# Three rounded products for one full-fp32 product of probabilities and values in a two-layer transformer kernel

## The chip, the core and the metric

The kernel runs on one core of a Trainium2 chip, in one launch. The metric is the device time of that launch in microseconds (us). Engines are named as in the profile: PE (matrix products), PEld (its weight loads), DVE, ACT, POOL and SP (which issues nearly all DMAs here).

## The reference, cut to what matters

Two layers of a hybrid backbone act on 1024 latent and 256 context tokens, width 1024, in fp32. Each layer normalises, projects into three parallel groups of heads (latent attention with 6 heads, a state-space model, windowed attention with 6 query and 2 key-value heads), concatenates and projects back, then runs a gated MLP with a short convolution. The change touches the product of probabilities and values in the two attentions:

```python
s = jnp.einsum('bqhd,bkhd->bhqk', qb, keys).astype(F32) * (MLA_QK ** -0.5)
p = jax.nn.softmax(s, axis=-1).astype(vals.dtype)
return jnp.einsum('bhqk,bkhd->bqhd', p, vals)
...
p = jax.nn.softmax(jnp.concatenate([s_sink, s_ctx, s_band], axis=-1), axis=-1).astype(v.dtype)
out = (jnp.einsum('bngrql,blgd->bnqgrd', p[..., 1:1 + n_ctx], v_ctx)
       + jnp.einsum('bngrqk,bnkgd->bnqgrd', p[..., 1 + n_ctx:], vb))
```

## The kernel before, in words

Tokens are 10 tiles of 128 (8 latent, 2 context) or 3 chunks (512, 512, 256). Nearly all large products are made of three passes in a rounded fp32 type (`mm3`, L88): each operand is held as a rounded part (hi) and the rest (lo), and hi·hi, hi·lo and lo·hi are accumulated. `split` (L124) makes the pair: ACT copies into the rounded type, DVE subtracts. The one large product that is a single full-fp32 matmul is that of probabilities and values, called av.

Per layer the order is: projections, state inputs (the loop that writes `us`, before L1839), latent attention, windowed attention, output projection, MLP.

*Latent attention* runs over 6 heads x chunks (L1851). `mla_prep` (L1436) loads a head's keys (`kn`, two buffers), queries and values (`v1`, straight into a tile whose 65th column is one, so that av also gives the softmax's denominator), transposes keys and queries on PE, splits them and takes row maxima on DVE. `mla_steps` (L1531) is one step per key tile: three score passes on PE into a PSUM tile `s` (three buffers), the exponential on ACT into `p` (fp32, four buffers), and a closure that does the av product. The closures wait in the list `pend`, so the product of a step is issued two steps later. Between steps, generators are advanced by a share: preparation of the next unit, the state-space work (`s5`, L1103, whose due times are weighed by a meter, and which is spread over five sixths of the steps), the modulation rows, and then the setup of the windowed attention (`swa_setup`, L1566, and `swa_prep`, L1621). Layer 0 has 6 x (10 + 10 + 2) = 132 steps, layer 1 has 6 x 20 = 120.

*Windowed attention* (`swa_steps`, L1723) works the same way on 384 columns (3 query heads x 128 tokens): 84 steps in layer 0, 76 in layer 1. Its setup loads masks, keys, values and queries; the tag `n2` has two buffers. During it, the mixed inputs of the output projection are loaded and split (`mix_loads`, L1765), and the first output weights (`wo_loads`, L1787; two sets in layer 0).

POOL only does the power of the normalisations (`rsqrt_pool`, L206) and a few memsets. The framework gives each engine its instructions in an order of its own choice near the program's order, and inserts the semaphores; a tile of a tag with n buffers waits until the tile n before it is no longer used. Elementwise and ACT instructions carry the line of a helper (L55), products L86, transposes L96, so groups are told apart by the names of the tiles: `p<-s`, `sp<-s` the exponentials, `av<-p,v` and `av<-sp,sv` the products, `s` the scores, `b` preparation and state space, `u`, `d`, `dx` the MLP, `o` the output projection.

Of the kernel before, what the change touches and what calls it, by code (L numbers as in the profile page):

```python
# [18 lines left out]
T = TL + TX  # L19
# [13 lines left out]
def trunk(ctx, tc, x, c, ctxt, c_ctx, w_mod, b_mod, norm1, w_in, q_lora_g, w_uq, kv_lora_g, w_ukv,  # L33
# [54 lines left out]
    def mm3(out, L, R, start, stop):  # L88
        mm(out, L[0], R[0], start, False)
        mm(out, L[0], R[1], False, False)  # L90
        mm(out, L[1], R[0], False, stop)

# [660 lines left out]
    for l in range(2):  # L753
# [662 lines left out]

        v1s, khs = [], []
        for i in range(2):
            v1 = ap.tile([128, NT, 65], F32, name=f"v1_{i}")
            G.memset(v1[:, :, 64:65], 1.0)  # L1420
            v1s.append(v1)
# [14 lines left out]
        def mla_prep(h, ci):  # L1436
# [3 lines left out]
            if ci == 0:  # L1440
                kn = ap.tile([128, NT, 96], F32, tag="kn", name="kn", bufs=2)
# [3 lines left out]
            if ci == 0:  # L1445
                v1 = v1s[h % 2]
                nc.sync.dma_start(out=v1[:, :, 0:64], in_=vd[h].rearrange("t p d -> p t d"))
# [3 lines left out]
                for t4 in range(0, NT, 4):  # L1451
# [6 lines left out]
                    yield  # L1458
# [72 lines left out]
        def mla_steps(h, ci):  # L1531
# [4 lines left out]
            if h % 2 == 0 and ci == 0:  # L1536
                pair["num"] = ap2.tile([128, T], F32, tag="num", name="num", bufs=2)
                pair["den"] = ap2.tile([128, T], F32, tag="den", name="den", bufs=2)
# [3 lines left out]
            for kt in kts:  # L1542
# [5 lines left out]
                p = ap.tile([128, 512], F32, tag="p", name="p", bufs=4)  # L1548
                act(p[:, :n], ps[:, :n], AF.Exp, scale=96.0 ** -0.5)

                def av(kt=kt, p=p):
# [3 lines left out]
                    mm(av[0:65, :n], v1[:, kt, :], p[:, :n], kt == kts[0], kt == kts[-1])  # L1555
# [10 lines left out]
        def swa_setup():  # L1566
# [3 lines left out]
            mask = swp.tile([128, 2, 128], F32, name="mask")  # L1570
            nc.sync.dma_start(out=mask, in_=k_mask)
            mask_r = swp.tile([128, 2, 128], F32R, name="mask_r")
            V.tensor_copy(mask_r, mask)
            ident_r = swp.tile([128, 128], F32R, name="ident_r")
            V.tensor_copy(ident_r, ident)
            bandm = swp.tile([128, 3, 128], F32R, name="bandm")
            V.tensor_copy(bandm[:, 0, :], mask[:, 1, :])
            ts(bandm[:, 1, :], ones, 0.0)
            V.tensor_copy(bandm[:, 2, :], mask[:, 0, :])
# [10 lines left out]
            swa.update(mask_r=mask_r, ident_r=ident_r, bandm=bandm, sink=sink, sinkrow=sinkrow)  # L1590
            qbs = []
            for i in range(2):
                qb = swp.tile([128, 1536], F32R, name=f"qb_{i}")
                V.tensor_copy(qb[64:128, :], mask[64:128, 0, 0:1].to_broadcast([64, 1536]))
# [3 lines left out]
            for kv in range(2):  # L1598
                k2 = swp.tile([128, 12, 2, 64], F32, tag="n2", name="k2", bufs=2)
                nc.sync.dma_start(out=k2[:, 0:NT], in_=skd[kv].rearrange("t p z d -> p t (z d)"))  # L1600
                v1 = swp.tile([128, NT, 65], F32, name=f"sv1_{kv}")
                G.memset(v1[:, :, 64:65], 1.0)
# [620 lines left out]
```

## Time and profile before

| | us |
|---|---|
| median of 3 runs | 3303.49 (3299.19 to 3305.27) |
| the profiled execution | 3301.99 |
| its span, first to last instruction | 3300.2 |
| busy PE / DVE / ACT / POOL | 3213.9 / 2206.6 / 1165.6 / 108.5 |

The profile is one execution. Its own time lies 1.5 us below the median of the runs. PE's matmuls are pipelined and their ends are modelled, so starts tell more than durations. A matmul in full fp32 appears as two records, each with its own weight load. The four stretches of attention in this execution: latent attention of layer 0 from 297.6 to 671 us (A0) and of layer 1 from 2053 to 2366 (A1), windowed attention from 671 to 788 (B0) and from 2366 to 2470 (B1).

### The profile page before, as it was taken

How to read it: one execution, taken by the hardware profiler on the slowest of the kernel's cores; microseconds unless marked ns; L12 is line 12 of the kernel's file. 1: busy time of each engine (PE TensorE's matmuls, PEld its weight loads, DVE VectorE, ACT ScalarE, POOL GpSimd, SP SyncE). 2: the span in 40 equal slices, each digit the busy share in tenths (PEclk: the TensorE clock that was granted, in tenths of full speed). 3: DMA queues.
4: the chain of work that ended last, by engine and by line, in shares of the span. 5: the costliest groups of instructions: out<-in, count | busy, mean ns of one | idle time of the engine just before them, and what ended most of it. 6: DMA issues, size and time to landing. Idle time of an engine off the chain costs nothing.

```text
span 3300.2 us, 42307 instructions
## 1 busy us (share of the span) xinstructions
PE 3213.9 (97%) x16150; PEld 2577.4 (78%) x16150; DVE 2206.6 (67%) x3987; ACT 1165.6 (35%) x2110; POOL 108.5 (3%) x99
## 2 busy tenths in 40 slices
PE   7999899999999999999999999999999999999999
PEld 4997566677888888888888898556668788888888
DVE  6657887775787766666666845987554756555565
ACT  4532444564232222222222453445562322222221
POOL 0220000000000000000000122000000000000000
PEclk9999899999999999999999999899999999999999
DMA  8534221434312222222211445111323111111111
GB/s 267 130 96 105 87 72 45 125 94 152 96 61 62 73 68 76 64 66 74 68 61 45 127 110 142 29 44 35 90 73 119 33 52 58 45 39 58 52 39 58
DMA packets 405731, 263.15 MB, mean 80 GB/s; under 512 B 173455, under 2 KB 378393, under 8 KB 405529
## 3 DMA queue, kind: packets, MB, share of 16 engines
q1 hardware_dynamic: 404882, 260.20, 27.2%
q8 instruction: 127, 2.08, 0.3%
q14 instruction: 75, 0.61, 0.1%
q10 hardware_dynamic: 647, 0.26, 0.0%
HBM read 207.41 MB, written 50.66 MB: 78 GB/s over the span
## 4 chain that ended last, share of the span: by engine, by line
PE 83%; DVE 10%; DMA 3%; ACT 2%; issue 1%; SPq 1%; POOL 1%; DVEq 0%; ACTq 0%; POOLq 0%
PE u L86 33%; PE d L86 11%; PE av L86 7%; PE o L86 5%; PE dx L86 5%; PE f L86 5%; PE s L86 5%; PE tk L86 5%; PE b L86 4%; PE b L96 2%; DVE cm L55 1%; DVE mx L55 1%; DMA raw<-md 1%; DVE al L55 1%; POOL rinv L102 1%
## 5 line engine op out<-in xcount | busy, mean ns | idle before, releaser
L86 PE MATMUL u<-ah,wh 128*128 128x512 f32 (+1 forms) x1760 | 649.7, 370 | 4.0 <-ACT ah L55 2.2
L86 PE MATMUL u<-al,wh 128*128 128x512 f32 (+1 forms) x1760 | 649.0, 369 | 1.7 <-DVE al L55 1.7
L86 PE MATMUL u<-ah,wl 128*128 128x512 f32 (+1 forms) x1760 | 648.4, 368 | 0.0
L55 ACT ACTIVATE wh<-raw 128x1024 fp32r<-128x1024 f32 (+3 forms) x184 | 189.3, 1036 | 739.8 <-PE d L86 292.1
L55 DVE SCALAR_TENSOR_TENSOR cv<-u,par,cv 128x511 f32<-128x511 f32 (+2 forms) x616 | 326.0, 555 | 133.5 <-ACT cv L55 128.4
L86 PEld LDWEIGHTS u<-ah,wh 128*128 128x128 f32 x1760 | 331.9, 189 | 60.5 <-ACT ah L55 3.1
L86 PEld LDWEIGHTS u<-al,wh 128*128 128x128 f32 x1760 | 332.2, 189 | 58.2 <-DVE al L55 2.8
L86 PEld LDWEIGHTS u<-ah,wl 128*128 128x128 f32 x1760 | 332.2, 189 | 55.2
L55 DVE TENSOR_TENSOR wl<-raw,wh 128x1024 fp32r<-128x1024 f32 (+3 forms) x184 | 218.3, 1191 | 179.0 <-ACT wh L55 177.8
L55 DVE SCALAR_TENSOR_TENSOR x<-d,g,x 128x512 f32<-128x512 f32 (+2 forms) x307 | 209.5, 685 | 109.2 <-PE d L86 108.9
L55 ACT ACTIVATE cv<-u,par,par 128x512 f32<-128x512 f32 (+1 forms) x220 | 159.7, 728 | 322.3 <-PE u L86 319.9
L86 PE MATMUL av<-p,v 128*65 128x512 f32 (+1 forms) x504 | 255.8, 590 | 1.2 <-ACT den L55 0.8
L86 PE MATMUL d<-ah,wh 128*128 128x512 f32 (+2 forms) x614 | 224.5, 366 | 1.3 <-DVE x L55 1.2
L86 PE MATMUL d<-al,wh 128*128 128x512 f32 (+2 forms) x614 | 223.5, 364 | 0.0
L86 PE MATMUL d<-ah,wl 128*128 128x512 f32 (+2 forms) x614 | 223.4, 364 | 0.0
L55 ACT ACTIVATE p<-s 128x512 f32<-128x512 f32 (+1 forms) x252 | 147.6, 586 | 195.9 <-PE s L86 190.8
L55 DVE TENSOR_REDUCE mx<-b 128x1 f32<-128x512 f32 (+1 forms) x300 | 164.4, 586 | 44.9 <-PE b L86 43.4
L55 DVE SCALAR_TENSOR_TENSOR macc<-mw,srow,macc 128x256 f32<-128x256 f32 (+1 forms) x308 | 147.5, 503 | 67.3 <-DMA mw<-in_w_mod_dram 66.9
L86 PE MATMUL s<-qh,kh 97*128 97x512 f32 (+1 forms) x252 | 159.8, 634 | 0.2 <-DMA qh<-nr 0.2
L86 PE MATMUL av<-sp,sv 128*65 128x384 f32 x320 | 127.4, 487 | 7.0 <-ACT sp L55 3.6
L86 PEld LDWEIGHTS d<-ah,wh 128*128 128x128 f32 x614 | 115.8, 189 | 20.8 <-DVE x L55 2.9
L55 DVE SCALAR_TENSOR_TENSOR x<-dx,g,x 128x512 f32<-128x512 f32 (+2 forms) x141 | 97.2, 690 | 51.4 <-PE dx L86 51.4
(354 smaller groups left out, 6137.7 us busy)
## 6 DMA issues: line engine op xcount, KB each, us to landing
raw<-in_w_up_dram SPq DMA_DIRECT2D x88, 512.0 KB
mw<-in_w_mod_dram SPq DMA_DIRECT2D x224, 128.0 KB
raw<-in_w_down_dram SPq DMA_DIRECT2D x44, 512.0 KB
wm<-in_w_mod_dram SPq DMA_DIRECT2D x16, 512.0 KB
xd<-x SPq DMA_DIRECT2D x32, 256.0 KB
mw<-in_w_mod_dram SPq DMA_DIRECT2D x16, 512.0 KB
raw<-in_w_in_dram SPq DMA_DIRECT2D x14, 512.0 KB
sqd<-sqb SPq DMA_DIRECT2D x36, 192.0 KB
```

The lines of the kernel that those rows point to most:

```text
L55: return fn(out, *args, **kw)
L86: PE.matmul(out, lhsT, rhs, start=start, stop=stop)
L96: PE.transpose(out, in_, ident[0:p, 0:p])
L102: (eng or V).tensor_tensor(out, a, b, op=op)
```

## The change

Values are loaded into a raw tile and split into a rounded part and a rest; the exponential still writes fp32, then ACT copies it into the rounded type and POOL subtracts the rounded part. The av product becomes three passes, the rest of the probabilities last. The list of waiting products grows from two to three. The key tile has one buffer, shared with the raw values; in the windowed setup mask, keys, raw values and queries share one buffer; the denominators have one buffer; the separate mask in the rounded type goes, since the banded one holds the same; the state inputs are staged in the weight pool's raw tiles; one set of output weights less is loaded ahead in layer 0 and one more after the windowed pools close.

```diff
+    def mm3r(out, L, R, start, stop):
+        mm(out, L[1], R[0], start, False)
+        mm(out, L[0], R[0], False, False)
+        mm(out, L[0], R[1], False, stop)
...
+        def val_tiles(pl, name):
+            vh, vl = (pl.tile([128, NT, 65], F32R, name=f"{name}{z}") for z in "hl")
+            V.tensor_copy(vh[:, :, 64], ones[:, 0:NT])
+            ts(vl[:, :, 64], ones[:, 0:NT], 0.0)
+            return vh, vl
+        def load_vals(v, raw, src):
+            nc.sync.dma_start(out=raw, in_=src.rearrange("t p d -> p t d"))
+            split(v[0][:, :, 0:64], v[1][:, :, 0:64], raw)
+        def probs(ps, n, scale):
+            p = pp.tile([128, 512], F32, tag="p", name="p", bufs=2)[:, :n]
+            hi = pp.tile([128, 512], F32R, tag="ph", name="ph", bufs=4)[:, :n]
+            lo = pp.tile([128, 512], F32R, tag="pl", name="pl", bufs=3)[:, :n]
+            act(p, ps, AF.Exp, scale=scale)
+            act(hi, p)
+            sub(lo, p, f32(hi), G)
+            return hi, lo
...
-                kn = ap.tile([128, NT, 96], F32, tag="kn", name="kn", bufs=2)
+                kn = ap.tile([128, NT, 96], F32, tag="kn", name="kn")
...
-                nc.sync.dma_start(out=v1[:, :, 0:64], in_=vd[h].rearrange("t p d -> p t d"))
...
-                    yield
+                    if t4 < 8:
+                        yield
+                raw = ap.tile([128, NT, 96], F32, tag="kn", name="vn")[:, :, 0:64]
+                load_vals(v1, raw, vd[h])
+                yield
...
-                pair["den"] = ap2.tile([128, T], F32, tag="den", name="den", bufs=2)
+                pair["den"] = ap2.tile([128, T], F32, tag="den", name="den")
...
-                p = ap.tile([128, 512], F32, tag="p", name="p", bufs=4)
-                act(p[:, :n], ps[:, :n], AF.Exp, scale=96.0 ** -0.5)
+                p = probs(ps[:, :n], n, 96.0 ** -0.5)
...
-                    mm(av[0:65, :n], v1[:, kt, :], p[:, :n], kt == kts[0], kt == kts[-1])
+                    mm3r(av[0:65, :n], (v1[0][:, kt, :], v1[1][:, kt, :]), p, kt == kts[0], kt == kts[-1])
...
-                k2 = swp.tile([128, 12, 2, 64], F32, tag="n2", name="k2", bufs=2)
+                k2 = swp.tile([128, 12, 2, 64], F32, tag="n2", name="k2")
...
-                nc.sync.dma_start(out=v1[:, :, 0:64], in_=svd[kv].rearrange("t p d -> p t d"))
+                v1 = val_tiles(swp, f"sv1_{kv}")
+                raw = swp.tile([128, 12, 2, 64], F32, tag="n2", name="v2")[:, 0:NT, 0, :]
+                load_vals(v1, raw, svd[kv])
...
-            q2 = swp.tile([128, 12, 2, 64], F32, tag="n2", name="q2", bufs=2)
+            q2 = swp.tile([128, 12, 2, 64], F32, tag="n2", name="q2")
...
-                        mm(ps, swa["ident_r"], swa["mask_r"][:, mk:mk + 1, :].to_broadcast([128, 3, 128]), False, True)
-                    p = swp.tile([128, 384], F32, tag="p", name="sp", bufs=4)
-                    act(p, ps, AF.Exp, scale=0.125)
+                        mm(ps, swa["ident_r"], swa["bandm"][:, 2 - 2 * mk:3 - 2 * mk, :].to_broadcast([128, 3, 128]), False, True)
+                    p = probs(ps, 384, 0.125)
...
-                        mm(av[0:65], v1[:, kt, :], p, e == 0, last)
+                        mm3r(av[0:65], (v1[0][:, kt, :], v1[1][:, kt, :]), p, e == 0, last)
...
-            for m in range(2 if need_ctx else 4):
+            for m in range(1 if need_ctx else 4):
...
-                us = ap.tile([128, 512], F32, tag="p", name="us", bufs=4)
+                us = W.raw()
...
+        pp, close_pp = open_pool("probs", side=sd)
...
-                if len(pend) == 2:
+                if len(pend) == 3:
...
-        w2_close = W.open("w2", 2, 1, side=sd)
+        w2_close = W.open("w2", 3 if need_ctx else 2, 1, side=sd)
```

## Rows read from the trace of the kernel before

**Rows 1.** The page: busy share of the engines, and the chain by engine.

```profile
PE 3213.9 (97%) x16150; PEld 2577.4 (78%) x16150; DVE 2206.6 (67%) x3987; ACT 1165.6 (35%) x2110; POOL 108.5 (3%) x99
...
PE 83%; DVE 10%; DMA 3%; ACT 2%; issue 1%; SPq 1%; POOL 1%; DVEq 0%; ACTq 0%; POOLq 0%
```

**Rows 2.** Windows A0, B0, A1, B1, next stage: length, busy PE, PEld, DVE, ACT, POOL.

```profile
297.60:671.00 373.40, 352.87 (x1831) 228.90 (x1830) 292.75 (x641) 179.04 (x379) 1.75 (x18) 0.96 0.27 76
671.00:788.00 117.00, 112.18 (x536) 80.87 (x535) 79.56 (x185) 75.85 (x163) 0.00 (x0) 1.00 0.34 99
2053.00:2366.00 313.00, 299.37 (x1338) 187.96 (x1337) 244.12 (x422) 153.75 (x304) 1.75 (x18) 0.97 0.20 50
2366.00:2470.00 104.00, 100.46 (x465) 72.23 (x464) 55.47 (x111) 66.45 (x136) 0.00 (x0) 1.00 0.28 81
788.00:850.00 62.00, 61.40 (x342) 53.45 (x341) 39.23 (x62) 11.74 (x17) 0.00 (x0) 1.00 0.66 211
```

**Rows 3.** Chain by line, first in A0, then in A1 (cut by the view).

```profile
by line: PE av L86 20.7%; PE b L86 18.6%; PE s L86 17.6%; PE b L96 7.2%; DVE cm L55 6.8%; DVE mx L55 3.5%; DVE pm L55 2.6%; issue 2.1%; ACT sv L55 2.0%; DVE u L55 1.8%; DVE Sg L55 1.7%; DVE sv L55 1.6%; DVE q L55 1.4%; DMA k<-skd 1.2%; DVE 
...
by line: PE av L86 19.2%; PE b L86 16.2%; PE s L86 15.2%; PE b L96 10.0%; DVE mx L55 4.6%; DVE cm L55 4.4%; DVE sv L55 3.9%; issue 2.9%; DVE u L55 2.1%; DVE pm L55 1.9%; DVE t L55 1.5%; DMA k<-skd 1.5%; SPq L1143 1.4%; DVE z L55 1.4%; DVE q
```

**Rows 4.** Lines by form on PE, whole run: count | busy us, mean ns | idle before.

```profile
L86 PE MATMUL av<-p,v 128*65 128x512 f32 x480 | 248.7, 600 | 0.4 <-issue 0.4
...
L86 PE MATMUL av<-sp,sv 128*65 128x384 f32 x320 | 127.4, 487 | 7.0 <-ACT sp L55 3.6 <-ACT sden L55 3.3
```

**Rows 5.** Timeline of PE in A0 and B0: start us, us, engine, instruction.

```profile
620.40 0.39 PE L86 MATMUL s<-qh,kl 96*128 96x512 f32 x1
...
620.63 1.02 PE L86 MATMUL av<-p,v 128*65 128x512 f32 x2
...
621.09 0.80 PE L86 MATMUL s<-qh,kh 97*128 97x512 f32 x1
...
621.73 0.40 PE L86 MATMUL s<-ql,kh 96*128 96x512 f32 x1
...
703.61 0.81 PE L86 MATMUL av<-sp,sv 128*65 128x384 f32 x2
703.96 0.63 PE L86 MATMUL s<-qa,ka 128*128 128x384 f32 x1
704.43 0.33 PE L86 MATMUL s<-qb,kb 128*128 128x384 f32 x1
704.60 0.34 PE L86 MATMUL s<-mask_r,ident_r 128*128 128x384 f32 x1
```

**Rows 6.** Lines by form on ACT in B0: the rounding copies there now.

```profile
L55 ACT ACTIVATE ah<-raw 128x512 fp32r<-128x512 f32 x10 | 6.3, 631 | 2.5 <-DMA raw<-md 2.4
...
L55 ACT ACTIVATE ah<-raw 128x256 fp32r<-128x256 f32 x5 | 2.1, 413 | 1.0 <-DMA raw<-md 1.0
```

**Rows 7.** Lines by form on DVE, whole run: the subtraction of a rounded part.

```profile
L55 DVE TENSOR_TENSOR al<-raw,ah 128x512 fp32r<-128x512 f32 x12 | 8.2, 685 | 3.7 <-ACT ah L55 3.7
```

**Rows 8.** Timeline of POOL's power, alone and beside DVE's subtractions.

```profile
122.72 2.27 POOL L102 TENSOR_TENSOR rinv<-ssq,mhalf 128x12 f32<-128x12 f32 x1 [5.36 <-DVE ssq L55]
...
219.23 1.22 DVE L55 TENSOR_TENSOR wl<-raw,wh 128x1024 fp32r<-128x1024 f32 x1
...
219.45 3.12 POOL L102 TENSOR_TENSOR rinv<-ssq,mhalf 128x12 f32<-128x12 f32 x1 [4.57 <-DVE ssq L55]
...
1917.57 2.35 DVE L55 TENSOR_TENSOR wl<-raw,wh 128x1024 fp32r<-128x1024 f32 x2
...
1917.80 4.25 POOL L102 TENSOR_TENSOR rinv<-ssq,mhalf 128x12 f32<-128x12 f32 x1 [0.81 <-DVE ssq L55]
```

**Rows 9.** Lines by form on DVE in A0.

```profile
L55 DVE TENSOR_REDUCE mx<-b 128x1 f32<-128x512 f32 x87 | 57.8, 682 | 24.7 <-PE b L86 24.3
L55 DVE TENSOR_REDUCE mx<-b 128x1 f32<-128x256 f32 x56 | 22.8, 413 | 0.5 <-PE b L86 0.3
L55 DVE TENSOR_TENSOR cm<-pm 128x640 f32<-128x640 f32 x16 | 19.5, 1240 | 0.0
...
L55 DVE TENSOR_TENSOR t<-E,sv 128x640 f32<-128x640 f32 x16 | 12.8, 816 | 2.3 <-ACT sv L55 2.3
```

**Rows 10.** The longest waits for loads on A0's chain: start us, us.

```profile
621.75 4.59 DMA k<-skd
```

More of the change, by code (lines that the diff above doesn't have):

```diff
@@ L1415, in all_mods @@
                 yield from mod_rows(ll, nm, mpl, bbank)
+        def val_tiles(pl, name):
[14 more added lines that the diff above has]
+            return hi, lo
         v1s, khs = [], []
         for i in range(2):
-            v1 = ap.tile([128, NT, 65], F32, name=f"v1_{i}")
-            G.memset(v1[:, :, 64:65], 1.0)
-            v1s.append(v1)
+            v1s.append(val_tiles(ap, f"v1_{i}"))
             kh = ap.tile([97, T], F32R, name=f"kh_{i}")
@@ L1569, in swa_setup @@
             swa["pool"] = swp
[L1570 to L1573, printed above, removed]
             ident_r = swp.tile([128, 128], F32R, name="ident_r")
@@ L1576, in swa_setup @@
             bandm = swp.tile([128, 3, 128], F32R, name="bandm")
+            mask = swp.tile([128, 12, 2, 64], F32, tag="n2", name="mask").rearrange("p a b c -> p (a b c)")
+            mask = mask[:, 0:256].rearrange("p (a b) -> p a b", a=2)
+            nc.sync.dma_start(out=mask, in_=k_mask)
             V.tensor_copy(bandm[:, 0, :], mask[:, 1, :])
+            V.tensor_copy(bandm[:, 2, :], mask[:, 0, :])
             ts(bandm[:, 1, :], ones, 0.0)
-            V.tensor_copy(bandm[:, 2, :], mask[:, 0, :])
             sink = swp.tile([128, 6], F32, name="sink")
@@ L1589, in swa_setup @@
                                   in_=bass.AP(sk.tensor, sk.offset, [[0, 2], [1, 3], [1, 1]]))
-            swa.update(mask_r=mask_r, ident_r=ident_r, bandm=bandm, sink=sink, sinkrow=sinkrow)
+            swa.update(ident_r=ident_r, bandm=bandm, sink=sink, sinkrow=sinkrow)
             qbs = []
@@ L1593, in swa_setup @@
                 qb = swp.tile([128, 1536], F32R, name=f"qb_{i}")
-                V.tensor_copy(qb[64:128, :], mask[64:128, 0, 0:1].to_broadcast([64, 1536]))
+                ts(qb[64:128, :], ones[64:128, 0:1].to_broadcast([64, 1536]), 0.0)
                 qbs.append(qb)
@@ L1598, in swa_setup @@
             for kv in range(2):
-                k2 = swp.tile([128, 12, 2, 64], F32, tag="n2", name="k2", bufs=2)
+                k2 = swp.tile([128, 12, 2, 64], F32, tag="n2", name="k2")
                 nc.sync.dma_start(out=k2[:, 0:NT], in_=skd[kv].rearrange("t p z d -> p t (z d)"))
-                v1 = swp.tile([128, NT, 65], F32, name=f"sv1_{kv}")
-                G.memset(v1[:, :, 64:65], 1.0)
-                nc.sync.dma_start(out=v1[:, :, 0:64], in_=svd[kv].rearrange("t p d -> p t d"))
+                v1 = val_tiles(swp, f"sv1_{kv}")
+                raw = swp.tile([128, 12, 2, 64], F32, tag="n2", name="v2")[:, 0:NT, 0, :]
+                load_vals(v1, raw, svd[kv])
                 ka = swp.tile([128, T], F32R, name=f"ka_{kv}")
@@ L1900, in trunk @@
                     loads.share(cnt - 16, 50)
-                if len(pend) == 2:
+                if len(pend) == 3:
                     pend.pop(0)()
@@ L1910, in trunk @@
                     apool, close_a = open_pool("A", side=other(sd))
-                    w1_close = W.open("w1", 2 if need_ctx else 4, 1, side=other(sd))
+                    w1_close = W.open("w1", 1 if need_ctx else 4, 1, side=other(sd))
                     mt = act_tiles(apool, qchunks)
@@ L1916, in all_loads @@
                         yield from wo_loads()
-                    loads = Side(all_loads(), 17 if need_ctx else 14)
+                    loads = Side(all_loads(), 16 if need_ctx else 14)
         for fin in pend:
@@ L1926, in trunk @@
         swa["close_mod"]()
+        close_pp()
         close_cps()
         sd = other(sd)
-        w2_close = W.open("w2", 2, 1, side=sd)
+        w2_close = W.open("w2", 3 if need_ctx else 2, 1, side=sd)
         xs, close_x = open_x(other(sd))
```

## The prediction

> **What bounds the kernel now.** I read the page's busy shares and chain first, then cut the span into stages with the table by windows, then went to single lines. Over the whole span PE is busy 97% and carries 83% of the chain, while POOL is 3% busy [rows 1]. Taken alone that says: any PE time saved is time saved, and POOL is free. The change acts in four stretches only, and there the picture differs [rows 2]. Call them A0 and A1 (latent attention of layers 0 and 1, with the state-space work and preparation woven in) and B0 and B1 (windowed attention). PE's busy counts overlapping passes, so I price PE by the spacing of starts. In A0 and A1 no engine is full: DVE is busy 293 of 373 us and 244 of 313, ACT 179 and 154, and the chain goes through PE for about two thirds and through DVE for most of the rest [rows 2, 3]. In B0 and B1 PE runs nearly without a gap, with ACT at 76 of 117 us and 66 of 104 [rows 2]. The stage after B0 is full of PE work (61.4 of 62 us, the last row of [rows 2]), so what B0 gains or loses goes straight into the span.
>
> **PE's saving.** A product in full fp32 is two records: 480 for 240 products 512 wide, 320 for 160 products 384 wide [rows 4]. Wide 512: from the start of the av pair (620.63) to the start of the second score pass (621.73) 1.10 us go by, of which the score pass between takes 0.23, its spacing just before (620.40 to 620.63); so a product costs 0.87, and three rounded passes 3 x 0.23 = 0.69: 0.18 saved. Wide 384: 703.61 to 704.43 is 0.82, less 0.17 for the score pass (704.43 to 704.60), so 0.65 against 3 x 0.17 = 0.51: 0.14 saved [rows 5]. The 12 products 256 wide save next to nothing. By stage: A0 120 x 0.18 = 22 us, A1 22, B0 84 x 0.14 = 12, B1 76 x 0.14 = 11; 67 us in all, 2.0% of the span. That is the upper end of any gain. In A0 av stands on the chain for 20.7% of 373 = 77 us, of some 120 x 0.87 = 104; in A1 for 19.2% of 313 = 60 [rows 2, 3]. So about 74% and 58% of the saving is on the path: -16 and -13 us.
>
> **ACT's second pass.** Each probability tile gets a rounding copy, SBUF to SBUF. The nearest rows are the same copy elsewhere: 631 ns at 512 columns, 413 at 256, so 522 at 384 [rows 6]. In A0 this is 120 x 0.63 + 12 x 0.41 = 81 us, which lifts ACT from 179 to 260 of 373; in A1 76, from 154 to 230 of 313. There is room, but ACT works in order and the state-space and key pieces must now queue behind it: a copy is running 81/373 = 22% of the time, and a piece that meets one waits half of 0.63, so 0.07 us on average; at some 100 such pieces, half of them on the path, +3 us in each. In B the room is gone. B0: 75.9 + 84 x 0.52 = 119.6 us of ACT in a stage of 117; B1: 66.5 + 76 x 0.52 = 106.0 in 104 [rows 2, 6]. ACT becomes the bound there and PE's 12 and 11 us are lost. Waits for loads and for the products remain inside ACT's queue; I add 5 us each for them, of which no single row gives the size. B0 +8, B1 +7. Bounds: ACT without a gap +3 and +2; the old gaps kept in full (117 - 76 = 41) would give +44 and +40. I stay near the lower end, since most of the old gaps are waits for PE, which is now ahead.
>
> **POOL's subtraction.** No row shows this operation on POOL. The same subtraction on DVE takes 0.69 us at 512 columns [rows 7]; that is the lower end. The only two-input operation of POOL is the power, 2.27 us for 12 elements undisturbed [rows 8]; at that price per element 512 would be near 100 us, a useless upper end. I take 1.3 us at 512 and 1.0 at 384 as an estimate, nearer to DVE's row since the work is the same, but about twice it, since no POOL row is quick. By it POOL is busy half of A and 84 of 117 us in B0, and a tile leaves it within the three steps by which the products now lag (the pending list grows from 2 to 3). The Trainium skill (GPSIMD Engine Reference, Performance versus the Vector engine) gives 4497 ns against 2293 for an addition 2048 wide; by that ratio, as an estimate, 512 columns are 1.35 us and the sum stays. What decides is whether it falls under the step: 117/84 = 1.4 us in B, 2.6 to 2.8 in A.
>
> **POOL against DVE.** The power operation took 2.27 us when DVE was quiet and 3.12 when a DVE subtraction of 1.22 with two SBUF inputs lay over its start; under two such in a row it took 4.25 [rows 8]. So the two engines exclude each other while both read SBUF, and here it was POOL that waited. The power reads 12 elements; the new subtraction reads for its whole length, so I expect DVE to wait when it comes second. No row shows that half. The price: in A0 the reductions out of PSUM are 58 + 23 us of DVE's 293, and most of the remainder are state-space operations with two SBUF inputs, of which two groups stand in [rows 9]; I estimate 135 us, 36% of the time. 132 subtractions x 36% x half of 1.3 us = 31 us of waiting, half of it on the path: +15. A1, with 120: +14. Bounds: 0 if DVE always goes first, and 132 x 1.3 x 36% = 62 and 56 us if each meeting costs the full length.
> The Trainium skill (SBUF — State Buffer, Who interferes with whom) says that a DVE instruction with two SBUF inputs contends with a GpSimd instruction that reads SBUF, and whoever comes second is blocked for the whole instruction. The rows bear out the half in which POOL waits; by the rule the 29 us stand, by the rows alone they are between 0 and that.
>
> **Smaller edits.** Values now pass through a raw tile and a split: 16 loads more of ACT and DVE work of about 0.8 us each, spread over the preparation a whole unit ahead of use; a unit is 10 steps of 2.6 us, so I cost it at nothing. The key tile goes from two buffers to one and is shared with the values, so each value load sits on SP's queue until the last key transposes are done; what stands behind it there are loads needed units later. If that cover were gone, it is one load of the kind on the chain (4.59 us) [rows 10] per head, 12 in all. In the windowed setup mask, keys, values and queries all share one buffer, so six loads of up to 4.6 us come one after another; the last sixth of A's steps covers most of it: +2 in layer 0, +1 in layer 1, at most +10 each. One output weight fewer is loaded ahead in layer 0, so its load and split begin only when the windowed pools close: +3, between 0 and 8. A single denominator buffer, the mask from another tile and the state inputs staged in the weight pool's raw tile: 0.
>
> **Sum.** A0 -16 + 3 + 15 = +2; A1 -13 + 3 + 14 = +4; B0 +8; B1 +7; setup +3; weights +3; together +27 on the profiled execution's 3302.0, so 3329.0. The median of the runs is 1.5 us above that execution: 3330.5.
>
> **The rivals.** (1) *PE's saving arrives.* DVE always goes first and POOL's waits vanish in the three steps of lag; ACT's copies fall into its gaps without delaying anything. A0 -16, A1 -13, B0 +3, B1 +2 by ACT's bare sum, the weights +3: -21, so 3282; if ACT too were hidden, the full 67 would give 3236. For it: the rows show DVE undisturbed at 1.22. Against it: ACT's sum in B is arithmetic. This is the case on the other side; it decides where waits of DVE in A stay under some 10 us. Chance 0.30. (2) *POOL becomes the bound.* If the subtraction with its waits costs more than the step of B, say 1.8 us at 384 wide, B0 and B1 become 84 x 1.8 = 151 and 76 x 1.8 = 137, +34 and +33, and A's waits reach about their bound on the path, +30 each: 3302 + 67 + 60 - 29 + 12 = 3412, with 12 for ACT's queueing and the smaller edits. Against it: it needs nearly three times DVE's price. Chance 0.13. (3) *Gain and loss cancel* within 0.2% (6.6 us, about what a measurement of this kernel can tell from no change). Chance 0.13. The forecast, ACT full in B and A given back to DVE's waits: 0.44.
>
> **How the numbers follow.** Faster is rival 1, 0.30; same 0.13; slower is the forecast and rival 2, 0.57. The range reaches down to 3270, past rival 1's own sum but not to the full saving, and up to 3392, which takes in the upper bounds of DVE's wait and ACT's gaps in part. The forecast's own range is 3312 to 3365.
>
> **What would show it.** Right: av with three records of about 0.17 or 0.23 spacing per product; ACT busy over 95% in both B stages, which grow to about 125 and 111 us; in A the two-input DVE instructions stretched or started late beside POOL, with DVE's busy or idle time up by tens of us, and A0 and A1 within a few us of 373 and 313. Wrong: A0 and A1 shorter by 15 us or more (DVE not held up), B shorter than now (ACT work moved out of the stage), or POOL subtractions of 1.8 us and more with PE waiting on them.

## The result and the profile after

Before 3301.98 us median (3299.19 to 3305.27, 4 runs), after 3528.03 (3527.10 to 3530.29, 4 runs): ratio 1.068, 95% interval [1.0665, 1.0696]. The change made the kernel 6.8% slower. The forecast, 3330.5 us in a range of 3270 to 3392, had the sign and an eighth of the size. The sign was in part luck: 15 of the 27 us forecast were ACT in windowed attention, and DVE and GpSimd, which made most of the loss, were forecast at 29 us and cancelled by 29 us of gain on PE.

The profiled execution after has a span of 3526.1 us against 3300.2. The page of the changed kernel, busy time and the chain by engine, answers to [rows 1]:

```profile
PE 3253.3 (92%) x16562; PEld 2657.2 (75%) x16562; DVE 2379.4 (67%) x4017; ACT 1388.2 (39%) x2538; POOL 655.2 (19%) x503
...
PE 69%; DVE 15%; issue 6%; DMA 4%; ACT 3%; POOL 3%; SPq 0%; DVEq 0%; POOLq 0%; ACTq 0%
```

PE's share of the chain fell from 83 to 69%, DVE's rose from 10 to 15%. DVE has 30 instructions more than before, and 173 us more of busy time.

The stretches are cut here from the start of the first exponential to the end of the last, which is up to 4 us tighter than [rows 2] in A and within 1 us of them in B. Windows after: stretch, length, busy PE, PEld, DVE, ACT, POOL, granted clock, DMA; the four stretches, then two short pieces inside A0:

```profile
294.50:734.20 439.70, 351.17 (x1893) 247.94 (x1894) 361.72 (x636) 254.49 (x511) 196.27 (x147) 0.89 0.23 67
735.70:878.70 143.00, 121.91 (x676) 94.06 (x674) 102.81 (x201) 114.15 (x250) 88.52 (x84) 0.96 0.28 83
2190.80:2575.90 385.10, 309.44 (x1444) 217.04 (x1443) 316.81 (x433) 226.63 (x437) 183.90 (x135) 0.88 0.16 41
2577.60:2692.70 115.10, 102.46 (x548) 79.66 (x546) 59.43 (x113) 99.65 (x213) 79.26 (x76) 0.99 0.27 80
...
344.50:347.50 3.00, 2.42 (x10) 1.00 (x9) 2.93 (x4) 2.32 (x6) 3.00 (x3) 1.00 0.00 0
347.50:365.00 17.50, 3.24 (x22) 2.09 (x22) 9.87 (x33) 6.33 (x19) 0.83 (x2) 0.56 0.56 193
```

With the three kernels that carry the explanation (experiments 1, 2 and 6) the loss is split like this, in us, by the profiled executions. The third column brings, besides the split and the three passes, the raw values that share buffers and the third waiting product:

| stretch | before | buffers alone | + split, no subtraction | + subtraction, unread | after |
|---|---|---|---|---|---|
| A0 | 369.6 | 368.4 | 366.1 | 441.4 | 439.7 |
| B0 | 116.1 | 120.7 | 125.2 | 143.8 | 143.0 |
| end of B0 to A1 | 1267.0 | 1310.6 | 1311.4 | 1311.0 | 1312.1 |
| A1 | 309.1 | 315.6 | 319.1 | 377.1 | 385.1 |
| B1 | 104.9 | 106.5 | 103.1 | 115.4 | 115.1 |
| span | 3300.2 | 3350.9 | 3362.6 | 3520.6 | 3526.1 |

Two entries make nearly all of it: GpSimd's subtraction in the attention stretches (169 us from the third column to the last) and 44 us outside attention that come with the buffers.

**What the subtraction does to DVE.** Lines by form of the changed kernel: DVE in A0 (its first three answer to [rows 9]), then ACT ([rows 6]) and POOL over the whole run:

```profile
L55 DVE TENSOR_REDUCE mx<-b 128x1 f32<-128x512 f32 x88 | 58.4, 683 | 23.9 <-PE b L86 23.5
L55 DVE TENSOR_TENSOR cm<-pm 128x640 f32<-128x640 f32 x16 | 22.1, 1406 | 0.0
L55 DVE TENSOR_TENSOR t<-E,sv 128x640 f32<-128x640 f32 x16 | 16.9, 1070 | 2.4 <-ACT sv L55 2.4
L55 DVE SCALAR_TENSOR_TENSOR ql<-b,gcol,qh 96x512 fp32r<-96x512 f32 x10 | 7.4, 742 | 2.4 <-ACT qh L55 2.4
L55 DVE TENSOR_TENSOR pt<-prmJ,s 128x32 f32<-128x32 f32 x8 | 4.4, 590 | 0.1
...
L55 ACT ACTIVATE ph<-p 128x512 fp32r<-128x512 f32 x240 | 149.7, 628 | 5.0
...
L55 ACT ACTIVATE ph<-p 128x384 fp32r<-128x384 f32 x160 | 81.0, 521 | 3.0 <-PE av L86 0.5
...
L108 POOL TENSOR_TENSOR pl<-p,ph 128x512 fp32r<-128x512 f32 x240 | 366.9, 1537 | 490.9 <-ACT ph L55 332.6 <-PE av L86 77.0 <-PE s L86 29.3
L108 POOL TENSOR_TENSOR pl<-p,ph 128x384 fp32r<-128x384 f32 x160 | 170.3, 1076 | 90.4 <-ACT ph L55 47.7 <-PE av L86 29.0 <-PE b L86 6.3
```

The reductions out of PSUM are where they were (683 ns, 682 before), and so is a difference that takes one of its inputs from PSUM (`ql`, 742). Instructions that take both inputs from SBUF are longer: `t` 1070 for 816, `cm` 1406 for 1240, and the 32-element ones shown, 188 ns in the kernel without subtractions, take 590. The timeline after, start us and us, shows how:

```profile
301.73 3.97 POOL L108 TENSOR_TENSOR pl<-p,ph 128x512 fp32r<-128x512 f32 x3
301.91 2.58 DVE L55 TENSOR_TENSOR s<-s,s 128x32 f32<-128x32 f32 x4
...
302.81 0.40 PE L86 MATMUL av<-ph,v_0l 128*65 128x512 f32 x1
...
303.05 0.40 PE L86 MATMUL av<-ph,v_0h 128*65 128x512 f32 x1
...
303.28 0.39 PE L86 MATMUL av<-pl,v_0h 128*65 128x512 f32 x1
...
304.42 1.32 DVE L55 CAST s<-s 128x32 f32<-128x32 int32 x1
...
305.66 0.18 DVE L55 TENSOR_TENSOR prmJ<-s,s 128x32 f32<-128x32 f32 x1
305.77 0.18 DVE L55 TENSOR_SCALAR s<-s 128x32 f32<-128x32 f32 x1
...
306.03 2.66 POOL L108 TENSOR_TENSOR pl<-p,ph 128x512 fp32r<-128x512 f32 x2 [0.33 <-PE s L86]
...
306.10 1.28 DVE L55 TENSOR_TENSOR s<-prmJ,prm 128x32 f32<-128x32 f32 x1
...
1164.17 0.39 PE L86 MATMUL d<-ah,wl 128*128 128x512 f32 x1
1164.44 1.49 DVE L55 TENSOR_TENSOR th<-th,cv 128x1280 f32<-128x1280 f32 x1
1165.96 1.27 ACT L55 ACTIVATE ah<-th 128x1280 fp32r<-128x1280 f32 x1 [2.86 <-DVE th L55]
...
1167.28 0.50 PE L86 MATMUL dx<-ah,wh 128*128 128x512 f32 x1 [2.72 <-ACT ah L55]
```

While subtractions follow each other (301.73, 306.03), a DVE instruction that lasts 0.18 us at 305.66 lasts 1.28 at 306.10: it ends with the subtraction over it. PE meanwhile has most of what it needs: the three av passes start 0.24 and 0.23 us apart, 0.7 in all, as forecast from [rows 5]. So a burst of steps goes on while DVE's other work, state space and preparation, hardly moves; after the burst DVE has the arrears to do and PE waits. That is the second pair of windows: in 344.5 to 347.5 POOL is busy throughout and DVE gets 4 instructions through; in the 17.5 us after it DVE does 33 and PE is busy 3.24 us. PE's two long waits there are 6.8 us for ACT, which itself waits 5.2 us for DVE's state-space parameters (`prmJ`), and 7.5 us for a load (`mw`). That load stands on SP's queue behind the store of these parameters, which SP issues 58.5 us into A0 and, in the kernel before, 35.5; DVE is idle too, 6.9 us, until the parameters are read back. The arrears thus also cost through SP's queue.

Over A0, PE's idle time is 439.7 - 351.2 = 88.5 us, against 366.1 - 333.8 = 32.3 without the subtractions. Those 56 us, and 17 us by which PE's busy time is longer at a granted clock of 0.89 in place of 0.93, are the 73.6 us that the subtraction costs A0.

**What the buffers do.** Two places outside attention. The first is the output projection behind B0. The chain after: by line in A0 (cut by the view, answering to [rows 3]), then pieces as start us, us, what, behind B0 and in A1:

```profile
by line: issue 20.7%; PE b L86 11.8%; DVE mx L55 6.9%; PE s L86 5.7%; PE av L86 5.6%; DVE cm L55 4.9%; POOL pl L108 4.7%; DVE Sg L55 3.1%; PE b L102 2.8%; DVE s L55 2.6%; DVE sv L55 2.6%; DVE u L55 2.3%; DVE t L55 2.0%; DVE z L55 1.6%; DVE 
...
890.67 5.11 DMA raw<-in_w_out_dram
...
895.89 1.06 ACT wh L55
...
897.00 22.30 PE o L86 x120
...
921.15 3.19 DMA mw<-in_w_mod_dram
...
2233.81 4.43 DMA vn<-vd
...
2522.84 4.66 DMA k<-skd
...
2537.65 4.49 DMA k<-skd
```

In A0 PE's av fell from 20.7 to 5.6% of the chain, and what was spread over PE now goes through many small DVE groups (of the share called issue, 49 us are one piece that the view could not follow).

The last exponential of B0 ended at 878.7; PE's long run of `o` starts at 897.0, behind a load of output weights that the program issues only after the windowed pools are closed; PE waits 13.3 us for it. From the end of B0 to the first `u` it is 133.9 us after, 118.8 before. The second place is the MLP of layer 0, 926.0 us from the first `u` to the last against 899.8. The lines at 1164 in the timeline above show it: PE's down products (`d`, `dx`) stand right behind the up products whose activation they read, and wait 2.7 us while DVE and ACT finish it. This happens five times, 172 us apart, some 5 us each, of which the wait is about half. In the 926 us PE is idle 22.1 us (4.8 before) and busy 903.9 us (895.1 before), since behind three of the five waits the granted clock is at its lower level for a while: 0.67 from 1167.2 to 1172.3, where passes start 0.43 us apart in place of 0.23. PE's waits there, after (us in total, times, longest); before the change the same list has no wait of `d` or `dx` for `ah`:

```profile
PE d L86 <- ACT ah L55: 7.3, 3, 2.7
PE dx L86 <- ACT ah L55: 5.5, 2, 2.8
```

### The profile page after: what moved, and what is told of

Read it like the earlier page. It is cut to its first block, busy times and chain, and to the rows that moved or that the text cites. A ratio compares the mean times of both kernels' runs of the same rounds, so it can differ in the third digit from the quotient of the medians.

```text
span 3526.1 us, 44465 instructions
## 1 busy us (share of the span) xinstructions
PE 3253.3 (92%) x16562; PEld 2657.2 (75%) x16562; DVE 2379.4 (67%) x4017; ACT 1388.2 (39%) x2538; POOL 655.2 (19%) x503
## 4 chain that ended last, share of the span: by engine, by line
PE 69%; DVE 15%; issue 6%; DMA 4%; ACT 3%; POOL 3%; SPq 0%; DVEq 0%; POOLq 0%; ACTq 0%
PE u L86 31%; PE d L86 10%; PE o L86 5%; PE dx L86 5%; PE tk L86 4%; PE f L86 4%; PE b L86 3%; PE av L86 3%; POOL pl L108 2%; PE s L86 2%; DVE mx L55 2%; PE b L102 1%; DVE cm L55 1%; DVE Sg L55 1%; DVE sv L55 1%
## 5 line engine op out<-in xcount | busy, mean ns | idle before, releaser
L108 POOL TENSOR_TENSOR pl<-p,ph 128x512 fp32r<-128x512 f32 (+2 forms) x412 | 550.1, 1345 | 583.3 <-ACT ph L55 380.8
L55 ACT ACTIVATE p<-s 128x512 f32<-128x512 f32 (+2 forms) x412 | 224.3, 547 | 183.6 <-PE s L86 107.2
L55 DVE SCALAR_TENSOR_TENSOR x<-d,g,x 128x512 f32<-128x512 f32 (+2 forms) x307 | 209.9, 686 | 115.1 <-PE d L86 114.5
L108 POOL TENSOR_TENSOR rn<-nv,mhalf 128x4 f32<-128x4 f32 (+1 forms) x11 | 13.5, 1223 | 1264.2 <-DVE nv L55 1264.2
L55 ACT ACTIVATE ph<-p 128x512 fp32r<-128x512 f32 (+2 forms) x412 | 235.8, 580 | 8.4 <-PE av L86 0.5
L55 DVE SCALAR_TENSOR_TENSOR macc<-mw,srow,macc 128x256 f32<-128x256 f32 (+1 forms) x308 | 158.1, 538 | 60.2 <-DMA mw<-in_w_mod_dram 59.4
L86 PE MATMUL b<-kh,qh 96*128 96x512 f32 (+1 forms) x300 | 119.2, 434 | 75.2 <-DVE ql L55 26.8
L86 PEld LDWEIGHTS b<-kh,qh 96*128 96x128 f32 x300 | 61.8, 215 | 118.1 <-DVE mx L55 36.1
```

Of the source, the lines that this page charges most:

```text
L55: return fn(out, *args, **kw)
L86: PE.matmul(out, lhsT, rhs, start=start, stop=stop)
L108: (eng or V).tensor_tensor(out, a, b, op=op)
```

## The experiments

Three theories were to be told apart. *Turns*: DVE and GpSimd hold each other up while both read SBUF, and the late DVE work then starves PE. *Buffers*: single buffers, and the other instruction order that comes with them. *Dependence or ScalarE*: the products wait for a slow subtraction, or the 412 copies fill ACT.

**1. The buffers alone**, in the kernel before.

```diff
-kn = ap.tile([128, NT, 96], F32, tag="kn", name="kn", bufs=2)
+kn = ap.tile([128, NT, 96], F32, tag="kn", name="kn")
... (den, k2 and q2 likewise)
-us = ap.tile([128, 512], F32, tag="p", name="us", bufs=4)
+us = W.raw()
-for m in range(2 if need_ctx else 4):
+for m in range(1 if need_ctx else 4):
... (w1 of one set in layer 0 in place of two, w2 of three)
```

> The kernel before with only the change's buffers: keys, normalised inputs and denominators of one buffer, one weight set open ahead of the output projection (three after it), the S5 input staged in the weights' raw tile. No split, one fp32 product, nothing on GpSimd. Turns theory (GpSimd's subtractions and VectorE hold each other up, and PE then waits for late preparation): the attention stages stay within 10 us of before, and only what lies outside attention moves (the 45 us between the end of B0 and the start of A1 in the changed kernel): about 3345 us. Buffer theory (single buffers and the other instruction order they bring make the attention late): A0 and A1 are each 50 us or more above before, 3450 to 3530 us.

Measured 3351.87 us, ratio 1.0147 [1.0125, 1.0169]. Attention is within 6.6 us of before in each stretch; 43.6 us lie between B0 and A1. The buffer theory falls for attention; the sharing of a buffer by keys and raw values is not in this kernel, it comes with the next.

**2. No subtraction.**

```diff
-            lo = pp.tile(...)
-            sub(lo, p, f32(hi), G)
-            return hi, lo
+            return hi, hi
```

> The changed kernel without the 412 subtractions on GpSimd: the rounded probabilities stand in for the rest in the third product, so the rest of the probabilities is left out of the result while PE and ScalarE do the same work as in the changed kernel. Turns theory: the 183 us of the four attention stages go, the 45 us outside stay: 3310 to 3350 us, DVE busy in A0 back from 362 to about 293 us. Buffer theory: still 3480 us or more. ScalarE theory (the 412 extra copies and evictions in one queue make the steps late): still 3450 us or more.

Measured 3360.63 us, 1.0172 [1.0144, 1.02]: 10 us above the turns range, far below the others. A0's window:

```profile
301.50:667.60 366.10, 333.79 (x1889) 242.05 (x1890) 292.25 (x636) 250.75 (x510) 1.60 (x16) 0.93 0.28 79
```

DVE is back at 292 us with the same 636 instructions that take 362 in the changed kernel, and the 32-element ones of above are back at 188 ns:

```profile
L55 DVE TENSOR_TENSOR pt<-prmJ,s 128x32 f32<-128x32 f32 x8 | 1.2, 188 | 0.1
```

ACT keeps its copies (251 us), so that they are not what makes A0 late in the changed kernel. And PE's saving is not there: three passes in place of the fp32 product save 22 us of PE in A0 by the forecast's price, yet A0 is only 2.3 us shorter than with the buffers alone, and A1 is 3.5 longer. How much of the saving the copies took is not shown: no run has the three passes without them.

**3. The subtraction on DVE.**

```diff
-            sub(lo, p, f32(hi), G)
+            sub(lo, p, f32(hi))
```

> The changed kernel with the 412 subtractions on VectorE in place of GpSimd. Turns theory: VectorE pays about 0.69 us per 512 columns for itself (the al<-raw row), 83 us in A0 on 293 of 373 us, and becomes the bound of A0 and A1 there at about 390 us in place of 440; 3370 to 3420 us, and the small VectorE instructions (128x32) are back at 0.18 to 0.19 us. Buffer theory: 3500 us or more, as the buffers are the same.

Measured 3498.48 us, 1.0589 [1.0564, 1.0614]: a miss by 78 us, though not for the buffers, which experiment 1 had cleared. A0 took 425.5 us and not 390:

```profile
297.50:723.00 425.50, 361.01 (x1940) 254.12 (x1941) 374.27 (x782) 251.43 (x511) 1.59 (x16) 0.89 0.24 69
```

DVE's busy time rose by the 82 us that were computed, but the stretch does not end when DVE is full: DVE is busy 88% of it, and 59 us of the 82 came on top. The 32-element instructions are back at 0.19 us, as expected. By this, DVE's work was on the path already, but the run does not separate that from waits for the subtraction itself, which now stands in DVE's queue: in A0 the exponentials wait 44.1 us for it (25 times) and the products 14.0 us (11 times).

**4. A subtraction that nobody needs**, in the kernel before.

```diff
 act(p[:, :n], ps[:, :n], AF.Exp, scale=96.0 ** -0.5)
+dt = dpool.tile([128, 512], F32, tag="dt", name="dt")
+sub(dt[:, :n], p[:, :n], p[:, :n], G)
... (the same on 384 columns in the windowed attention)
```

> The kernel before with one dummy subtraction on GpSimd in each of the 412 steps (probabilities minus themselves into a tile that nobody reads); its result is not used, all else as before. Turns theory: the VectorE instructions beside it are stretched as in the changed kernel, A0 and A1 grow by 35 to 75 us each, total 3400 to 3490 us. Buffer theory, and the view that only the dependence of the third product on the subtraction matters: within 15 us of before.

Measured 3396.58 us, 1.028 [1.0252, 1.0309], 3 us under the range of the turns theory. A0 +51.0, A1 +37.9, both as it said. Nothing reads the result and the other tiles keep their buffers. In B it is otherwise, before and with the dummy:

```profile
670.40:786.50 116.10, 111.28 (x533) 80.53 (x532) 79.56 (x185) 76.31 (x164) 0.00 (x0) 1.00 0.34 100
722.60:842.90 120.30, 113.07 (x534) 80.18 (x533) 92.60 (x185) 76.36 (x164) 73.05 (x83) 1.00 0.32 97
```

DVE's busy time in B0 rises by 13.0 us and the stretch by 4.2: there DVE has room, and its held instructions cost little.

**5. The weight sets alone**, in the kernel before.

```diff
-for m in range(2 if need_ctx else 4):
+for m in range(1 if need_ctx else 4):
... (w1 of one set in layer 0 in place of two, w2 of three)
```

> The kernel before with only the change's weight sets: in layer 0 one set open ahead of the output projection and three opened after it, in place of two and two. Theory (the 43.6 us that the kernel with all the change's buffers lost outside attention come from these sets alone: 13.6 in the output projection, 26.3 in the MLP of layer 0, 3.7 behind it): 3341 to 3350 us, all four attention stages within 6 us of before. Rival (the staging tile of the S5 input or the single projection buffers move the order that far down): within 10 us of before.

Measured 3357.13 us, 1.0144 [1.0119, 1.0169], 7 us above the range. All four stretches are within 2.5 us of before, and from B0 to A1 it is 48.3 us more. PE's waits in the MLP of layer 0 are those of the changed kernel:

```profile
PE d L86 <- ACT ah L55: 8.4, 3, 3.5
PE dx L86 <- ACT ah L55: 5.5, 2, 2.8
```

So one set fewer ahead and one more behind cost the whole 44 us. Why the framework then puts the down products right behind their up products stays open; no run changes the one without the other.

**6. The subtraction stays, the product doesn't read it.**

```diff
             sub(lo, p, f32(hi), G)
-            return hi, lo
+            return hi, hi
```

> The changed kernel with its 412 subtractions on GpSimd, but the third product reads the rounded probabilities and not the subtraction's output, so that the rest of the probabilities is left out of the result and no product waits for GpSimd. Turns theory (it is VectorE's held-up instructions that cost): A0 stays 50 to 75 us and A1 40 to 66 us above the kernel without subtractions (366.1 and 319.1 us), total 3470 to 3530 us. Dependence theory (the products wait for a slow GpSimd): A0 and A1 within 15 us of it, total below 3400 us.

Measured 3523.80 us, 1.0655 [1.0627, 1.0683], 4 us from the changed kernel. The dependence theory falls: no product waits for GpSimd here, and the time is the same. The exponentials still do, for one of the two fp32 tiles that the subtraction frees (31.0 us in 35 waits in A0); experiment 12 tries that.

**7. GpSimd writes but doesn't read**, in the kernel before.

```diff
+G.memset(p[:, :n], 0.0)
 act(p[:, :n], ps[:, :n], AF.Exp, scale=96.0 ** -0.5)
```

> The kernel before with a GpSimd instruction in each of the 412 steps that writes and reads nothing: the tile of the probabilities is cleared ahead of the exponential. Port theory (VectorE is held only where its two inputs lie in SBUF and GpSimd reads SBUF): VectorE's 128x32 TENSOR_TENSOR instructions stay at 0.18 to 0.19 us beside it, A0 and A1 within 12 us of before, total 3295 to 3325 us, against 3397 us with the dummy subtraction. Rival (any GpSimd instruction in the steps costs, by its issue or its semaphores): 3370 to 3410 us.

Measured 3306.06 us, 0.9999 [0.9989, 1.001]. Lines by form, DVE in A0 and POOL over the run:

```profile
L55 DVE TENSOR_TENSOR cm<-pm 128x640 f32<-128x640 f32 x16 | 19.5, 1243 | 0.0
L55 DVE TENSOR_TENSOR pt<-prmJ,s 128x32 f32<-128x32 f32 x8 | 1.2, 187 | 0.1
...
L1549 POOL MEMSET p<- 128x512 f32 x240 | 127.9, 533 | 533.0 <-PE av L86 416.0 <-DMA ud<-us 37.6 <-PE b L86 20.4
```

412 GpSimd instructions in the same steps cost nothing, and DVE's instructions with two inputs are not longer. Some with one input are (copies, casts and TENSOR_SCALAR: 4.4 us in all over the run). The clears are shorter than the subtractions (0.53 us for 1.30 in experiment 4), so this alone does not rule out length, but experiment 9 has reading ones of 0.77 us that cost 36 us. The Trainium skill (SBUF — State Buffer, Who interferes with whom) states that a DVE instruction with two SBUF inputs contends with a GpSimd instruction that reads SBUF and not with one that only writes it. The runs agree: 3397 us with the reading dummy, 3306 with the writing one, and of DVE's forms those fed from PSUM were not lengthened.

**8. The rounded probabilities alone**, written by the exponential: no copy, no subtraction, two products; most buffers as before (the values still go through the keys' tiles, the state inputs through the weights').

```diff
-            act(p, ps, AF.Exp, scale=scale)
-            act(hi, p)
-            sub(lo, p, f32(hi), G)
-            return hi, lo
+            act(hi, ps, AF.Exp, scale=scale)
+            return hi
...
-        mm(out, L[1], R[0], start, False)
-        mm(out, L[0], R[0], False, False)
-        mm(out, L[0], R[1], False, stop)
+        mm(out, L[1], R, start, False)
+        mm(out, L[0], R, False, stop)
```

> The rounded probabilities written by the exponential itself, without copy and subtraction, and two products with the split values; the rest of the probabilities is left out of the result. Weight sets, keys, projections, denominators and pending steps as before. PE's product goes from 0.87 to 0.46 us at 512 columns and from 0.65 to 0.34 at 384, 148 us over the 412 steps. Theory (in A0 and A1 the bound is the chain through VectorE and PE's saving mostly does not arrive; in B0 and B1 it does): A0 and A1 5 to 20 us shorter each, B0 and B1 10 to 20 each, total 3235 to 3285 us. Rival (PE is the bound in all four): 3155 to 3200 us.

Measured 3258.27 us, 0.9854 [0.9835, 0.9874], less than both kernels. The total was in the range, but only B1 of its parts: A0 -26.4, B0 -3.1, A1 -3.5, B1 -14.7. Of 148 us that PE is spared, 48 arrived.

**9. Half the dummy**, in the kernel of experiment 4.

```diff
-sub(dt[:, :n], p[:, :n], p[:, :n], G)
+sub(dt[:, :n // 2], p[:, :n // 2], p[:, :n // 2], G)
```

> The kernel before with the dummy subtraction on GpSimd over half the columns (256 and 192 in place of 512 and 384) in each of the 412 steps; its result is not used. Turns theory (each held VectorE instruction waits as long as GpSimd reads, so that the price goes with the columns): A0 and A1 grow by half of what the full dummy cost, 18 to 32 and 12 to 25 us, total 3335 to 3362 us. Rival (each handover between the two engines has a fixed price, whatever the length): A0 and A1 as with the full dummy, total 3385 to 3400 us.

Measured 3339.82 us, 1.0104 [1.0078, 1.013]. A0 +17.7, just under its range, and A1 +13.7, in it. With half the columns an undisturbed dummy takes 0.61 us in place of 1.04, and the stretches grow by 35 and 36% of what the full one cost: the price goes with the length of the reading, and a fixed one for each handover is not seen. A0's windows of the kernel before at this cut, and of experiments 9, 4 and 6:

```profile
297.60:667.20 369.60, 349.07 (x1790) 226.28 (x1788) 292.01 (x639) 176.49 (x372) 1.75 (x18) 0.96 0.27 77
```

```profile
298.40:685.70 387.30, 355.86 (x1790) 228.57 (x1788) 311.45 (x639) 176.35 (x372) 114.18 (x149) 0.94 0.27 73
```

```profile
298.90:719.50 420.60, 364.93 (x1790) 233.29 (x1789) 344.73 (x639) 177.16 (x372) 167.75 (x149) 0.91 0.24 68
```

```profile
297.20:738.60 441.40, 352.32 (x1893) 251.43 (x1894) 359.30 (x636) 253.99 (x511) 199.38 (x147) 0.88 0.24 66
```

| against | POOL busy added in A0 | DVE busy added | A0 longer by | the same in A1: DVE, A1 |
|---|---|---|---|---|
| half dummy / before | 112 | 19 | 18 | 13, 14 |
| dummy / before | 166 | 53 | 51 | 35, 38 |
| unread / no subtraction | 198 | 67 | 75 | 61, 58 |
| after / no subtraction | 195 | 69 | 74 | 66, 66 |
| on DVE / no subtraction | 0 | 82 | 59 | 71, 51 |

In the four pairs with GpSimd the DVE instructions are the same in number: A0 and A1 grow by about a us for each us that DVE's instructions are longer.

**10. Two steps pending**, in the changed kernel.

```diff
-                if len(pend) == 3:
+                if len(pend) == 2:
```

> The changed kernel with two steps in flight behind the scores, as before, in place of three. Turns theory (VectorE's instructions set the time of A, not the products' wait for the subtraction): A0 and A1 within 10 us of the changed kernel, total 3515 to 3545 us. Rival (the third step in flight hides the 1.3 us of the subtraction): each of the 412 steps waits longer, total above 3570 us.

Measured 3543.21 us, 1.0719 [1.0691, 1.0747]. A0 +0.9, A1 -1.1: the third step hides nothing there. The 15 us are spread over B (+2.3, +2.6) and the rest.

**11. One product**, both factors rounded, in the kernel of experiment 8.

```diff
-        mm(out, L[1], R, start, False)
-        mm(out, L[0], R, False, stop)
+        mm(out, L[0], R, start, stop)
...
-            split(v[0][:, :, 0:64], v[1][:, :, 0:64], raw)
+            act(v[0][:, :, 0:64], raw)
```

> As the kernel with two products and the exponential writing the rounded probabilities, but one product: the values are rounded too, their rest is left out of the result as well, and VectorE makes no differences for the values. PE's product goes from 0.46 to 0.23 us at 512 columns and from 0.34 to 0.17 at 384, 85 us over the 412 steps. Theory (A0 and A1 bound by the chain through VectorE, B0 and B1 only partly by PE): 10 to 40 us below the kernel with two products (3258 us), 3218 to 3248 us. Rival (PE bounds the steps): 3170 to 3190 us.

Measured 3236.41 us, 0.9794 [0.9773, 0.9814], the shortest here and within the range. 22 of 85 us arrived. Windows, A0 and B0 of experiment 8, then of this one:

```profile
298.30:641.50 343.20, 311.82 (x1781) 229.05 (x1780) 293.41 (x638) 179.25 (x378) 1.60 (x16) 0.92 0.31 86
643.10:756.10 113.00, 99.43 (x572) 84.92 (x570) 84.24 (x199) 75.92 (x167) 0.00 (x0) 0.92 0.36 106
```

```profile
294.90:634.60 339.70, 292.57 (x1636) 215.11 (x1637) 285.49 (x623) 180.05 (x378) 1.59 (x16) 0.87 0.31 86
635.90:751.40 115.50, 93.88 (x503) 78.06 (x502) 87.47 (x207) 75.50 (x166) 0.00 (x0) 0.88 0.35 102
```

In A0 DVE stays at 285 to 293 us whatever PE is spared, and A0 moves by 3.5 us from the one to the other.

**12. Three tiles for the fp32 probabilities**, in the changed kernel. With four rounded tiles kept the pools do not fit: the state-space pool needs 99 kb per partition and 97.09 are left. So there are three of them.

```diff
-            p = pp.tile([128, 512], F32, tag="p", name="p", bufs=2)[:, :n]
-            hi = pp.tile([128, 512], F32R, tag="ph", name="ph", bufs=4)[:, :n]
+            p = pp.tile([128, 512], F32, tag="p", name="p", bufs=3)[:, :n]
+            hi = pp.tile([128, 512], F32R, tag="ph", name="ph", bufs=3)[:, :n]
```

> The changed kernel with three tiles in place of two for the full fp32 probabilities, which the exponential fills and GpSimd's subtraction frees, and, for the room, three in place of four for the rounded ones. Turns theory with a ring in B (in B0 and B1 VectorE has room, and the exponential waits until GpSimd frees one of two tiles): A0 and A1 within 10 us of the changed kernel (439.7 and 385.1), B0 and B1 each 6 to 16 us shorter than 143.0 and 115.1, total 3500 to 3520 us. Rival (B is late because ScalarE is full and VectorE held): B0 and B1 within 4 us, total 3522 to 3535 us.

Measured 3520.02 us, 1.0645 [1.0614, 1.0676]. B1 108.7 for 115.1, as the ring would have it, B0 140.1 for 143.0, as the rival would: not settled by this run. The exponentials' wait for GpSimd fell from 24.1 to 13.0 us in A0, which took 441.7 for 439.7, and from 20.1 to 5.2 in A1, which took 376.5 for 385.1. So it is not what makes A0 late, and in A1 8.6 of the 66 us came back.

## Why the prediction was wrong, step by step

- **PE's saving** (-16, -13): the price was right, 3 x 0.23 us for 0.87. That 74% and 58% of it would arrive, by av's share of the chain, was wrong: with the subtraction left out and the buffers discounted, A0 gained 2.3 us and A1 lost 3.5, ACT's copies included. An engine's share of the chain tells where the chain ran, not what is left when that piece shrinks. That DVE's chain was right behind is argued from experiments 4 and 11; how the loss divides between it, the copies and a lower granted clock (0.93 for 0.96 in A0) is not shown.
- **ACT's second pass**: 628 and 521 ns against 631 and 522. What it cost in A0 cannot be told from PE's saving: the two together were forecast at -13 us and came to -2.3. In B the forecast was 125 and 111 us with ACT over 95% busy; without the subtraction B0 is 125.2 (4.6 of the 9 us by the buffers alone) and B1 103.1, with ACT at 88 and 94%. So B0 came out right, half of it by luck, and B1 did not: +7 was forecast and it is 1.8 us shorter than before.
- **POOL's price**: 1.3 us at 512 columns against 1.28 for those with no DVE instruction beside them (1.54 in the mean, its own waits included), 1.0 at 384 against 1.01 and 1.08. Right. The ratio in the Trainium skill (GPSIMD Engine Reference, Performance versus the Vector engine) gave an estimate of 1.35 us, and the trace agrees with it.
- **POOL against DVE** is the step that failed. It read: "132 subtractions x 36% x half of 1.3 us = 31 us of waiting, half of it on the path: +15", with an upper bound of 62. The mechanism was right and both sizes were off. DVE's added time in A0 is 69 us, 0.53 us per subtraction and not 0.23. Against the median of its form in experiment 2, 79 DVE instructions are longer by over 0.15 us, by 0.87 us each: 60% as many as subtractions and not 36%, and held for 0.87 us and not 0.65. The 36% came from 135 us of work with two SBUF inputs, but the forms of the kernel before whose inputs are all in SBUF sum to 182 us in A0, 49%; and it takes the two engines to meet by chance, while in a burst the next subtraction starts at once and meets the next instruction of DVE's queue. And not half of it was on the path but, within a few us, all: +74 in A0, +66 in A1. The 62 us were no bound, because they kept the 36%.
- **The same step was not priced in B at all.** B0 grew by 17.8 us with the subtraction and its DVE busy time by 17 (85.6 to 102.8). Yet in experiment 4 another 13.0 us of DVE cost B0 only 4.2, so that DVE is not shown to be the cause there. In B1 DVE's grew by 3.5 and the stretch by 12.0, so that DVE is not the cause; a third fp32 tile took back 6.4 of it (experiment 12), where the exponentials had waited 10.2 us for GpSimd. The rest, in B0 nearly all, is open.
- **Smaller edits**: the single buffers were put at 3 us and cost 11 over the four stretches (A0 -1.2, B0 +4.6, A1 +6.5, B1 +1.6 with the buffers alone); the loads that show, one of values and two of keys of 4.4 to 4.7 us, stand in the chain of A1 above (a load of keys stood in the chain before too, [rows 3]). "One output weight fewer: +3, between 0 and 8" was the second failure: 44 us. The load behind B0 cost 14 in place of 3, and what the term left out was that the same sets serve the whole MLP of layer 0, in another order (+26).
- **The sum**: 29 us forecast for DVE and GpSimd, 169 measured over the four stretches; 3 forecast for the weights, 44 measured. PE's 29 us of gain in A did not show. Rival 2 (GpSimd the bound) is not what happened either: its price in B was 1.08 us in the mean and not 1.8, and A was late although no product had to wait for it. The rivals on the fast side needed PE's saving to arrive.

## What to carry to other kernels

Price work for an idle GpSimd by what it does to the engine beside it: where both read SBUF, count how many DVE instructions with inputs in SBUF stand in its time, and price each meeting at most of a GpSimd instruction (here 0.87 us of 1.28, for 60 meetings in 100 subtractions), above all where the GpSimd work comes in bursts. A stretch in which no engine is full can still be bound by one of them; the test is a dummy that lengthens that engine's work, and in A0 and A1 each us of it cost about a us. When a buffer is taken from a pool that later stages share, follow that pool to its last user before calling the edit small.

## What the runs showed of the hardware that was not expected

- DVE instructions with one SBUF input were held too: the CAST at 304.42 lasted 1.32 us for 32 elements (0.17 without subtractions), and of the two TENSOR_SCALAR `s<-s` of A0, 713 ns in the mean, one took 0.18 us (305.77) and so the other 1.25. A GpSimd instruction that only writes held some of them as well: beside the clears of experiment 7 two TENSOR_SCALAR `sink<-sink` of 6 elements took 0.57 us each, 0.16 before; the one at 618.11 ended with the clear over it. In the changed kernel reductions and differences out of PSUM were not (683 against 682 ns, 742 against 743).
- The granted TensorE clock was lower where PE was left waiting, which takes part of a saving back: in A0 0.96 before with 20.5 us of PE idle, 0.93 without subtraction with 32.3, 0.89 after with 88.5, 0.87 with one product and 47.1, where PE had the least to do. In the 17.5 us behind the burst, with PE busy 3.24, it was 0.56. These are means over the stretch, between its two levels of 1.2 and 2.4 GHz. B0 took 115.5 us with one product, at 0.88, and 113.0 with two, at 0.92.
